# Attention of a hybrid decoder layer: where the far products with values stand, and in which order the four tiles of a group run

## The chip, the core and the metric

The kernel runs on one core of a Trainium2 chip. The time is the device time of one execution in microseconds; of several executions the median is given. The profile is one execution, recorded by the hardware profiler: for each engine it tells when each instruction ran, what it wrote and read, and what it had waited for. The engines are TensorE (PE; its weight loads are kept apart as PEld), VectorE (DVE), ScalarE (ACT), GpSimd (POOL), and SyncE (SP), which here only issues DMAs. Each engine takes its instructions in the order in which they were written for it, and an instruction that waits holds up everything behind it on its engine.

## The reference

One decoder layer on 2048 tokens and 1024 channels: attention heads and pooling groups side by side, then a gated MLP, then a gated embedding, then a last normalisation. The change touches the attention alone: 8 heads of 64 channels, and for each head three dilated patterns whose outputs are mixed by their softmax denominators.

```
DIL_PATTERNS = ((128, 1), (512, 4), (2048, 16))      # (window, dilation)
...
    s = jnp.einsum('bnqrhd,bnkrhd->bnrhqk', qb, kk)
    ...
    s = s - slopes[:, None, None] * dist
    s = jnp.where(valid[:, None, None], s, -jnp.inf)
    m = jnp.max(s, axis=-1, keepdims=True)
    e = jnp.exp(s - m)
    den = jnp.sum(e, axis=-1)
    o = jnp.einsum('bnrhqk,bnkrhd->bnqrhd', e, vv)
    ...
w = d * jnp.exp(m - jnp.max(m, axis=0, keepdims=True))
w = w / jnp.sum(w, axis=0, keepdims=True)
return jnp.sum(w[..., None] * o, axis=0)
```

## The kernel before

The program has three phases: projections, attention, and the rest. All of the change lies in `phase_attention`.

The attention is worked off in 128 **steps**: 8 heads of 16 query tiles of 128 rows. Four tiles make a **group**, which shares one residue of the dilation by 4; a group has a far part (the two long patterns at once) and a near part (the short one). Tile i of a group (i from 0 to 3) sees i + 1 blocks of 128 far keys, so its far scores are 128, 256, 384 or 512 wide; its near scores are 256 wide (128 for the first tile of a head). In float32 each score is made of two products: `qhh` (upper part of the query) and `qll` (lower part).

For a step s, this happens, each item on one engine:

- `near_scores` (N) and `far_scores` (F): two PE products each, into `sn` and `sf`. The stationary operand of the near products is a run of 128 queries, that of the far products every fourth query (`t.qr`, `t.qlr`).
- `near_max`, `far_max` (nm, fm): DVE adds the distances and takes the row's extreme, from `sn` and `sf` into `tt`.
- `near_exp`, `far_exp` (ne, fe): ACT takes the exponentials, from `tt` into `ee`.
- `turn` (T): PE transposes `ee` block by block (near and far, 3 to 6 blocks) into `tp`.
- `high` (h): ACT copies `tp` into `pth`; `low` (l): DVE takes the remainder `tp` - `pth` into `ptl`.
- `values`, `values_b` (V, W): PE multiplies `pth` and `ptl` of a whole group with the values `v`, in four parts: far parts 0 and 1 (`far_pv`), near parts 2 and 3 (`near_pv`), each split in two halves V and W. Block kb of the far part is (4 - kb) x 128 wide: 512, 384, 256, 128.
- `fold` (o) on ACT copies the far output out of `o`, `folded` (p) on DVE the near one.

What is written for the engines in one pass of the step loop is set by a table of names and lags. In pass s, the item with lag k works for step s - k:

```
'ord': [B 0, G 0, M 0, h 2, N 0, F 0, nm 0, p 7, o 8, ne 0, V 6, fm 0, l 2, W 6, S 1, fe 0, T 1]
```

So in pass s PE gets N(s), F(s), the values V and W of six steps ago, and then T(s - 1); DVE gets nm(s), at times a copy p, then fm(s), then l(s - 2); ACT gets h(s - 2), at times a copy o, then ne(s), fe(s). All engines follow this written order; no planner reorders it. `CFG['perm']` tells which tile i of its group a step takes:

```
st.n = n = n - n % 4 + CFG["perm"][n % 4]
st.r, st.i = divmod(n, 4)
st.nb, st.nf = min(n, 1) + 1, st.i + 1
```

The accumulators lie in PSUM. `sf` has two buffers, `o` two, and `sn` one bank with two halves. `tp` comes from two pools of **one buffer each**, chosen by the number of far blocks:

```
def turn(s):
    st = steps[s]
    if st.nf > 2:
        st.tp = ps_t.tile([P, 1024], F32, tag="t", name="tp")
    else:
        st.tp = ps_t.tile([P, CH], F32, tag="u", name="tp")
```

A buffer may be written again once all that read it have done so: for `tp` that is h on ACT and l on DVE. Once for each of the first three pairs of heads, `mix_stats` (S, at lines 795 and 798) also takes a buffer of the tag "t", under the name `tps`.

Of the kernel before, what the change touches and what calls it, by code (L numbers as in the profile page):

```python
# [20 lines left out]
S = 2048  # L21
# [19 lines left out]
V_N = V_CB + 2 * NF  # L41


CFG = {"tt": 2, "ee": 2, 'ord': [['B', 0], ['G', 0], ['M', 0], ['h', 2], ['N', 0], ['F', 0], ['nm', 0], ['p', 7], ['o', 8], ['ne', 0], ['V', 6], ['fm', 0], ['l', 2], ['W', 6], ['S', 1], ['fe', 0], ['T', 1]], 'perm': [3, 1, 2, 0], 'fp': [[0], [1], [2], [3]], 'np': [[0, -1], [1], [2], [3]], 'm': [9, 10, 13, 4, 6, 7]}


class Shared:
# [444 lines left out]
def phase_attention(tc, g, mx, near_b, far_b):  # L492
# [4 lines left out]
    NS = H * NQ  # L497
    LAST = 4 * H - 2
    with ExitStack() as ctx:
# [6 lines left out]
        heads, steps, groups, pairs = {}, {}, {}, {}  # L506
# [35 lines left out]
        def begin(s):  # L542
# [7 lines left out]
            st = steps[s] = Shared()  # L550
            st.n = n = n - n % 4 + CFG["perm"][n % 4]
            st.t, st.pt, st.e = heads[h], pairs[h // 2], h % 2
# [5 lines left out]
            st.d1, st.d3 = st.pt.st1[:, 1, st.e, n : n + 1], st.pt.st3[:, st.r, 1, st.e, st.i : st.i + 1]  # L558
            st.tt = sb.tile([P, 768], F32, tag="tt", bufs=CFG["tt"], name="tt")
            st.ee = sb.tile([P, 768], F32, tag="ee", bufs=CFG["ee"], name="ee")  # L560

        def far_scores(s):
            st = steps[s]
            t = st.t
            st.fv = ps_f.tile([P, CH], F32, tag="f", name="sf")[:, : st.wf]
            keys = t.ks[:, : st.nf, st.r, :]
            cl = slice(st.i * P, (st.i + 1) * P)
            nc.tensor.matmul(st.fv, t.qr[:, st.r, cl], keys, start=True, stop=False)
            nc.tensor.matmul(st.fv, t.qlr[:, st.r, cl], keys, start=False, stop=True)

        def near_scores(s):
            st = steps[s]
            t, n = st.t, st.n
            if s == 0:
                near_bank.append(ps_n.tile([P, CH], F32, tag="n", name="sn"))
            st.nv = near_bank[0][:, (s % 2) * 256 : (s % 2) * 256 + st.wn]
            keys = tokens(t.ks, n) if st.nb == 1 else two_tiles(t.ks, n)
            qs = slice(n * P, (n + 1) * P)
            nc.tensor.matmul(st.nv, t.qhh[:, qs], keys, start=True, stop=False, skip_group_check=True)
            nc.tensor.matmul(st.nv, t.qll[:, qs], keys, start=False, stop=True, skip_group_check=True)  # L580
# [48 lines left out]
        def near_pv(gi, kbs, first):  # L629
            gr, q0 = groups[gi], 4 * (gi % 4)  # L630
            for kb in kbs:
                if q0 + kb < 0:
                    continue
                m0, m1 = max(0, kb), min(3, kb + 1)
                b0, b1 = 4 * m0 + kb + 1, 4 * m1 + kb + 1
                kt = q0 + kb
                for pt in (gr.h, gr.l):
                    nc.tensor.matmul(
                        gr.o[1][:, m0 * P : (m1 + 1) * P],
                        vals[gi // 8, "v1", kt // 4][:, kt % 4, gi // 4 % 2, :],  # L640
                        pt[:, b0 : b1 + 1 : 4, :],
                        start=first,
                        stop=False,
                        skip_group_check=True,
                    )
                    first = False

        def far_pv(gi, kbs, first):
            gr = groups[gi]
            for kb in kbs:  # L650
                for pt in (gr.h, gr.l):
                    nc.tensor.matmul(
                        gr.o[0][:, kb * P :],
                        vals[gi // 8, "v3", gi % 4][:, kb, gi // 4 % 2, :],
                        pt[:, 6 * kb + 2 : 18 + kb : 5, :],
                        start=first,
                        stop=False,
                        skip_group_check=True,
                    )
                    first = False  # L660

        sums = Ticker()

        def halves(pt, gi, near):
            h, q = divmod(gi, 4)
            e = h % 2
            mine = slice(DH * e, DH * e + DH)
            other = slice(DH * (1 - e), DH * (1 - e) + DH)
            return e, mine, other, pt.s1[:, q * CH : (q + 1) * CH] if near else pt.s3[:, q, :]
# [17 lines left out]
        def shifts(s):  # L687
            sums.tick()

        def values(v):  # L690
            gi, part = v // 4, v % 4
            gr = groups[gi]
            if part % 2 == 0:
                gr.__dict__.setdefault("o", []).append(ps_o.tile([P, CH], F32, tag="o", name="o"))
            if part < 2:
                far_pv(gi, CFG["fp"][2 * part], part == 0)
            else:
                near_pv(gi, CFG["np"][2 * part - 4], part == 2)

        def values_b(v):  # L700
            gi, part = v // 4, v % 4
            if part < 2:
                far_pv(gi, CFG["fp"][2 * part + 1], False)
            else:
                near_pv(gi, CFG["np"][2 * part - 3], False)

# [50 lines left out]
        with tc.manual_schedule(engines=set(EN.values())):  # L757
            for dst, src in load_qk(0):
                rdma(nc, dst, src)
            for q in range(4):  # L760
                for which in ("v3", "v1"):
                    rdma(nc, *load_v(0, which, q))
            queue = []
            stages = {
                "F": far_scores, "N": near_scores, "fm": far_max, "nm": near_max, "fe": far_exp, "ne": near_exp,
                "T": turn, "h": high, "l": low, "V": values, "W": values_b, "S": stats, "M": mix, "o": fold, "p": folded, "B": begin, "G": shifts
            }
            for s in range(NS + 10):
                if s < NS:
                    h, n = divmod(s, NQ)  # L770
# [1174 lines left out]
def tile_layer(ctx, tc, xT, pT, vec, w_in, pool_w, w_out, w_up, w_down, w_gate, w_ple, near_b, far_b, rcnt, outT, upto=9):  # L1945
# [44 lines left out]
    with tc.manual_schedule(engines={mybir.EngineType.PE}):  # L1990
        with tc.manual_schedule(engines={EN[e] for e in ACFG["man"]}):
            phase_project(tc, g, xT, w_in, pool_w, rcnt)
        if upto > 1:
            mxs = ExitStack()
            mx = mxs.enter_context(tc.tile_pool(name="b_mx", bufs=1, side="right", reuse_waits="tile"))
            last = phase_attention(tc, g, mx, near_b, far_b)
            if upto > 2:
                phase_rest(tc, g, mxs, mx, last, xT, pT, w_out, w_up, w_down, w_gate, w_ple, outT)
            else:
                mxs.close()  # L2000
# [71 lines left out]
```

## Time and profile before

| | |
|---|---|
| median of 3 runs | 2359.09 us (2354.91 to 2359.45) |
| profiled execution | 2356.13 us, span 2354.1 us |
| attention, first score product to last value product | 387.3 to 637.3 us, 250 us |
| in it: PE busy | 241.51 us |
| ACT busy | 227.83 us |
| DVE busy | 218.46 us |
| POOL busy | 143.74 us |
| mean granted TensorE clock in it | 0.99 |

"Busy" counts an instruction from its start to its end, so overlapping starts and ends on PE and ACT make an engine look a little fuller than it is. In rows of the timeline the first number is the start in microseconds from the start of the span, the second the duration; in square brackets stands how long the engine had been idle before, and what ended that.

### The profile page before, as it was taken

How to read it: one execution, taken by the hardware profiler on the slowest of the kernel's cores; microseconds unless marked ns; L12 is line 12 of the kernel's file. 1: busy time of each engine (PE TensorE's matmuls, PEld its weight loads, DVE VectorE, ACT ScalarE, POOL GpSimd, SP SyncE). 2: the span in 40 equal slices, each digit the busy share in tenths (PEclk: the TensorE clock that was granted, in tenths of full speed). 3: DMA queues.
4: the chain of work that ended last, by engine and by line, in shares of the span. 5: the costliest groups of instructions: out<-in, count | busy, mean ns of one | idle time of the engine just before them, and what ended most of it. 6: DMA issues, size and time to landing. Idle time of an engine off the chain costs nothing.

```text
span 2354.1 us, 32813 instructions
## 1 busy us (share of the span) xinstructions
PE 2307.5 (98%) x11279; PEld 1955.0 (83%) x11279; DVE 1697.9 (72%) x2663; ACT 1125.0 (48%) x2044; POOL 571.9 (24%) x568
## 2 busy tenths in 40 slices
PE   8999999999899999999999999999999999999998
PEld 7988888999878878888887888888778888888888
DVE  6735436888863778999999999777765656655665
ACT  5423325999821344445446444444454544544332
POOL 2312221367600233333330665000110000001000
PEclk9999999999999999999999999999999999999999
DMA  8635446778764764555667777444496776754332
GB/s 263 209 121 192 152 157 236 249 242 272 225 235 156 251 209 151 200 192 194 205 199 258 272 275 249 154 137 152 167 344 223 253 230 199 236 161 148 119 103 95
DMA packets 237575, 476.00 MB, mean 202 GB/s; under 512 B 34400, under 2 KB 60832, under 8 KB 234336
## 3 DMA queue, kind: packets, MB, share of 16 engines
q1 hardware_dynamic: 205040, 394.64, 50.8%
q0 software_dynamic: 15888, 51.69, 6.2%
q10 hardware_dynamic: 16480, 27.58, 3.3%
q8 instruction: 89, 1.46, 0.3%
q14 instruction: 78, 0.64, 0.1%
HBM read 309.14 MB, written 156.79 MB: 198 GB/s over the span
## 4 chain that ended last, share of the span: by engine, by line
PE 86%; DVE 5%; DMA 4%; issue 2%; ACT 2%; POOL 1%; SPq 0%; DVEq 0%; POOLq 0%; ACTq 0%
PE ua L1405 18%; PE uc L1405 9%; PE dn L90 5%; PE dn L89 5%; PE dn L91 5%; PE z L89 5%; PE z L90 5%; PE z L91 5%; PE ub L1405 5%; PE o L91 2%; PE o L89 2%; PE o L90 2%; PE tp L610 2%; PE gp L89 2%; PE gp L90 2%
## 5 line engine op out<-in xcount | busy, mean ns | idle before, releaser
L90 PE MATMUL dn<-al,wu 128*128 128x512 f32 x616 | 240.3, 390 | 2.4 <-DVE al L85 2.4
L89 PE MATMUL dn<-ah,wu 128*128 128x512 f32 x616 | 240.4, 390 | 0.2
L91 PE MATMUL dn<-ah,wu 128*128 128x512 f32 x616 | 239.8, 389 | 0.0
L85 DVE TENSOR_TENSOR al<-ra,ah 128x512 fp32r<-128x512 f32 x154 | 105.7, 689 | 111.4 <-ACT ah L84 111.1
L89 PE MATMUL z<-hnh,wh 128*128 128x512 f32 (+1 forms) x480 | 168.4, 351 | 7.9 <-ACT hnh L258 6.2
L90 PE MATMUL z<-hnl,wh 128*128 128x512 f32 (+1 forms) x480 | 167.9, 350 | 0.1
L91 PE MATMUL z<-hnh,wl 128*128 128x512 f32 (+1 forms) x480 | 167.5, 349 | 0.0
L84 ACT CAST ah<-ra 128x512 fp32r<-128x512 f32 x154 | 95.2, 621 | 147.1 <-PE dn L91 137.6
L90 PEld LDWEIGHTS dn<-al,wu 128*128 128x128 f32 x616 | 115.6, 188 | 27.8 <-DVE al L85 4.1
L89 PEld LDWEIGHTS dn<-ah,wu 128*128 128x128 f32 x616 | 115.6, 188 | 25.4 <-ACT ah L84 1.3
L91 PEld LDWEIGHTS dn<-ah,wu 128*128 128x128 f32 x616 | 115.6, 188 | 23.9
L85 DVE TENSOR_TENSOR wu<-ru,wu 128x1024 fp32r<-128x1024 f32 x88 | 135.0, 1534 | 0.0
L1405 PE MATMUL ua<-s4h,wu 128*128 128x512 f32 x352 | 118.4, 398 | 0.0
L1405 PE MATMUL uc<-s3h,wu 128*128 128x512 f32 x352 | 116.7, 392 | 1.5 <-ACT s3h L1461 1.5
L1405 PE MATMUL ua<-s2h,wu 128*128 128x512 f32 x352 | 116.1, 391 | 1.7 <-ACT ug L1607 1.5
L1405 PE MATMUL ua<-s1h,wu 128*128 128x512 f32 x352 | 115.7, 389 | 1.6 <-ACT ug L1633 1.6
L1405 PE MATMUL ua<-a11h,wu 128*128 128x512 f32 x352 | 115.7, 390 | 0.0
L1405 PE MATMUL uc<-a22h,wu 128*128 128x512 f32 x352 | 115.6, 389 | 0.0
L1405 PE MATMUL ub<-a12h,wu 128*128 128x512 f32 x352 | 115.5, 389 | 0.0
L85 DVE TENSOR_TENSOR wu<-rw,wu 128x512 fp32r<-128x512 f32 x149 | 100.8, 685 | 20.1 <-ACT wu L84 19.8
L155 DVE TENSOR_TENSOR acc<-acc,sq 128x512 f32<-128x512 f32 (+1 forms) x118 | 79.1, 670 | 41.8 <-ACT sq L154 30.5
L89 PEld LDWEIGHTS z<-hnh,wh 128*128 128x128 f32 x480 | 92.4, 192 | 20.0 <-ACT hnh L258 6.2
(339 smaller groups left out, 6638.6 us busy)
## 6 DMA issues: line engine op xcount, KB each, us to landing
ru<-in_w_up_dram SPq DMA_DIRECT2D x66, 512.0 KB, 4.2
wr<-in_w_in_dram SPq DMA_DIRECT2D x64, 256.0 KB, 5.0
rw<-in_w_down_dram SPq DMA_DIRECT2D x61, 256.0 KB, 4.2
nt<-h SPq DMA_DIRECT2D x56, 256.0 KB, 3.9
td<-t SPq DMA_DIRECT2D x22, 512.0 KB, 2.6
t<-td SPq DMA_DIRECT2D x22, 512.0 KB, 3.7
nt<-in_w_down_dram POOLq DMA_DIRECT2D x44, 256.0 KB, 5.6
ra<-oq0s SPq DMA_DIRECT2D x44, 256.0 KB, 3.5
```

The costliest lines, as they stand in the source:

```text
L84: nc.scalar.copy(hi, src)
L85: (low or nc.gpsimd).tensor_tensor(lo, src, fp(hi), op=ALU.subtract)
L89: nc.tensor.matmul(ps, wh, ah, start=first, stop=False, skip_group_check=again)
L90: nc.tensor.matmul(ps, wh, al, start=False, stop=False, skip_group_check=again)
L91: nc.tensor.matmul(ps, wl, ah, start=False, stop=last, skip_group_check=again)
L155: nc.vector.tensor_tensor(acc[:, :n], acc[:, :n], sq[:, :n], op=ALU.add)
L610: nc.tensor.transpose(st.tp[:, bs], st.ee[:, bs], g.ident)
L1405: nc.tensor.matmul(pst, x[:, ksl], y, start=first and k == 0 and n == 0, stop=k == HK - 1 and n == 2, skip_group_check=True)
```

## The change

The diff does three things. First, the order of the four tiles: `perm` was 3, 1, 2, 0 and is now 3, 2, 0, 1. By the step's number modulo 4 the far scores were 512, 256, 384, 128 wide and are now 512, 384, 128, 256 wide, and the `tp` buffers, which went t, u, t, u, now go t, t, u, u. Second, the far value blocks are paired anew: part 0 had the blocks of 512 and 384 columns, part 1 those of 256 and 128; now part 0 has 512 and 128, part 1 has 384 and 256. Third, the V half of a far part no longer stands at its own place behind F: its two products are written between those of F, value, score, value, score.

```diff
-'perm': [3, 1, 2, 0], 'fp': [[0], [1], [2], [3]],
+'perm': [3, 2, 0, 1], 'fp': [[0], [3], [1], [2]],
...
         def far_scores(s):
...
+            v = s - 6
+            with_values = 0 <= v < NS and v % 4 < 2
+            between = values(v, True) if with_values else iter(())
+            next(between, None)
             nc.tensor.matmul(st.fv, t.qr[:, st.r, cl], keys, start=True, stop=False)
+            next(between, None)
             nc.tensor.matmul(st.fv, t.qlr[:, st.r, cl], keys, start=False, stop=True)
+            if with_values:
+                assert next(between, None) is None
+                taken.add(v)
...
         def far_pv(gi, kbs, first):
...
                     first = False
+                    yield True
...
-        def values(v):
+        def values(v, steps=False):
+            if v in taken:
+                return
             gi, part = v // 4, v % 4
...
             if part < 2:
-                far_pv(gi, CFG["fp"][2 * part], part == 0)
+                it = far_pv(gi, CFG["fp"][2 * part], part == 0)
+                if steps:
+                    return it
+                list(it)
```

Since V and W have a lag of 6, far part 0 falls on steps with s modulo 4 = 2, and part 1 on those with 3. `turn` itself is as before.

On PE, a step with remainder 2 in the middle of head 1, from its near scores to the transposes of the step ahead of it. Before:

```order
L579 MATMUL sn_4007<-ks1_4019,qhh1_4017 128x256 [waits DVE_49]
L580 MATMUL sn_4007<-ks1_4019,qll1_4018 128x256
L568 MATMUL sf_4542<-ks1_4019,qhh1_4017 128x384
L569 MATMUL sf_4542<-ks1_4019,qll1_4018 128x384
L652 MATMUL o_4550<-pth_4432,v3_0_0_3985 128x512 [waits Activation_49]
L652 MATMUL o_4550<-ptl_4433,v3_0_0_3985 128x512 [waits DVE_49]
L652 MATMUL o_4550<-pth_4432,v3_0_0_3985 128x384
L652 MATMUL o_4550<-ptl_4433,v3_0_0_3985 128x384
L610 MATMUL tp_4558<-ident_60,ee_4508 128x128 [waits PE_49,Activation_49]
```

and now:

```order
L587 MATMUL sn_4007<-ks1_4019,qhh1_4017 128x256 [waits DVE_49]
L588 MATMUL sn_4007<-ks1_4019,qll1_4018 128x256
L660 MATMUL o_4543<-pth_4432,v3_0_0_3985 128x512 [waits Activation_49]
L572 MATMUL sf_4542<-ks1_4019,qhh1_4017 128x128
L660 MATMUL o_4543<-ptl_4433,v3_0_0_3985 128x512 [waits DVE_49]
L574 MATMUL sf_4542<-ks1_4019,qll1_4018 128x128
L660 MATMUL o_4543<-pth_4432,v3_0_0_3985 128x128
L660 MATMUL o_4543<-ptl_4433,v3_0_0_3985 128x128
L618 MATMUL tp_4558<-ident_60,ee_4508 128x128 [waits DVE_49,PE_49]
```

The values now stand around the scores, the scores are the narrowest instead of the second widest, and the first transpose, which waited for PE and ACT, now waits for DVE.

On DVE, the items of that step and of the one behind it (`ISA` is nm or fm; its row with `128x1` reads the extreme out). Before:

```order
L584 ISA tt_4991,st1_4803<-sn_4007,nb2_4399 128x256 [waits DVE_49,PE_49]
L584 ISA st1_4803 128x1
L676 COPY ev_5003<-o_4948 128x512 [waits DMAHW5_49,Pool_49]
L590 ISA tt_4991,st3_4804<-sf_4999,fb2_4400 128x384 [waits PE_49]
L590 ISA st3_4804 128x1
L627 TENSOR_TENSOR ptl_4995<-tp_4982,pth_4994 128x768 [waits Activation_49]
L584 ISA tt_5021,st1_4803<-sn_4007,nb2_4399 128x256 [waits DVE_49,PE_49]
L584 ISA st1_4803 128x1
L590 ISA tt_5021,st3_4804<-sf_5027,fb2_4400 128x128 [waits PE_49]
L590 ISA st3_4804 128x1
L627 TENSOR_TENSOR ptl_4995<-tp_5015,pth_4994 128x512 [waits Activation_49]
```

and now:

```order
L592 ISA tt_4991,st1_4802<-sn_4007,nb2_4399 128x256 [waits DVE_49,PE_49]
L592 ISA st1_4802 128x1
L686 COPY ev_5006<-o_4946 128x512 [waits DMAHW5_49,Pool_49]
L598 ISA tt_4991,st3_4803<-sf_4999,fb2_4400 128x128 [waits PE_49]
L598 ISA st3_4803 128x1
L635 TENSOR_TENSOR ptl_4995<-tp_4982,pth_4994 128x768 [waits Activation_49]
L592 ISA tt_5022,st1_4802<-sn_4007,nb2_4399 128x256 [waits DVE_49,PE_49]
L592 ISA st1_4802 128x1
L598 ISA tt_5022,st3_4803<-sf_5028,fb2_4400 128x256 [waits PE_49]
L598 ISA st3_4803 128x1
L635 TENSOR_TENSOR ptl_4995<-tp_5015,pth_4994 128x640 [waits Activation_49]
```

DVE's order of items is as it was; only the widths follow the tiles. The last item of the first step (its sixth row) reads `tp` of the tile with four far blocks (768 columns), as before.

On PE, the end of a step with remainder 0: the last near values, then the transposes. Before:

```order
L638 MATMUL o_4493<-ptl_4323,v1_0_2_3995 128x128
L638 MATMUL o_4493<-pth_4322,v1_0_3_3999 128x256
L638 MATMUL o_4493<-ptl_4323,v1_0_3_3999 128x256
L610 MATMUL tp_4503<-ident_60,ee_4460 128x128 [waits DVE_49,PE_49,Activation_49]
L610 MATMUL tp_4503<-ident_60,ee_4460 128x128 [waits Activation_49]
```

and now:

```order
L646 MATMUL o_4491<-ptl_4323,v1_0_2_3995 128x128
L646 MATMUL o_4491<-pth_4322,v1_0_3_3999 128x256
L646 MATMUL o_4491<-ptl_4323,v1_0_3_3999 128x256
L618 MATMUL tp_4501<-ident_60,ee_4461 128x128 [waits DVE_49,PE_49]
L618 MATMUL tp_4501<-ident_60,ee_4461 128x128
```

The work ahead of the transposes is the same. The transposes' buffer was "u", last used two steps before, and is "u" again, now last used one step before.

More of the change, by code (lines that the diff above doesn't have):

```diff
@@ L41 @@
 V_N = V_CB + 2 * NF
-CFG = {"tt": 2, "ee": 2, 'ord': [['B', 0], ['G', 0], ['M', 0], ['h', 2], ['N', 0], ['F', 0], ['nm', 0], ['p', 7], ['o', 8], ['ne', 0], ['V', 6], ['fm', 0], ['l', 2], ['W', 6], ['S', 1], ['fe', 0], ['T', 1]], 'perm': [3, 1, 2, 0], 'fp': [[0], [1], [2], [3]], 'np': [[0, -1], [1], [2], [3]], 'm': [9, 10, 13, 4, 6, 7]}
+CFG = {"tt": 2, "ee": 2, 'ord': [['B', 0], ['G', 0], ['M', 0], ['h', 2], ['N', 0], ['F', 0], ['nm', 0], ['p', 7], ['o', 8], ['ne', 0], ['V', 6], ['fm', 0], ['l', 2], ['W', 6], ['S', 1], ['fe', 0], ['T', 1]], 'perm': [3, 2, 0, 1], 'fp': [[0], [3], [1], [2]], 'np': [[0, -1], [1], [2], [3]], 'm': [9, 10, 13, 4, 6, 7]}
 class Shared:
@@ L660, in far_pv @@
                     first = False
+                    yield True
         sums = Ticker()
+        taken = set()
         def halves(pt, gi, near):
@@ L702, in values_b @@
             if part < 2:
-                far_pv(gi, CFG["fp"][2 * part + 1], False)
+                list(far_pv(gi, CFG["fp"][2 * part + 1], False))
             else:
```

## The prediction

> **What bounds the kernel now.** I read the page first, then the attention's stretch by engine, then PE's, DVE's and PEld's timelines of one group.
>
> ```profile
> PE 2307.5 (98%) x11279; PEld 1955.0 (83%) x11279; DVE 1697.9 (72%) x2663; ACT 1125.0 (48%) x2044; POOL 571.9 (24%) x568
> 387.30:637.30 250.00, 241.51 (x1673) 232.25 (x1671) 218.46 (x694) 227.83 (x679) 143.74 (x139) 0.99 0.80 253
> ```
>
> PE is busy nearly all the time, in the attention too (241.51 of 250 us), but there DVE and ACT stand close behind. So a gain on PE counts at once, and a wait of PE on DVE costs at once. I call the steps by their number modulo 4 (step 2, 3, 0, 1), and a step's tile by the same number. One group on PE:
>
> ```profile
> 421.03 0.36 PE L579 MATMUL sn<-ks,qhh 128*128 128x256 f32 x1
> 421.23 0.28 PE L580 MATMUL sn<-ks,qll 128*128 128x256 f32 x1
> 421.35 0.45 PE L568 MATMUL sf<-ks,qhh 128*128 128x384 f32 x1
> 421.64 0.40 PE L569 MATMUL sf<-ks,qll 128*128 128x384 f32 x1
> 421.87 0.40 PE L652 MATMUL o<-pth,v 128*128 128x512 f32 x1
> 422.34 0.34 PE L652 MATMUL o<-pth,v 128*128 128x384 f32 x1
> 422.70 0.60 PE L610 MATMUL tp<-ident,ee 128*128 128x128 f32 x4
> ...
> 423.05 0.30 PE L579 MATMUL sn<-ks,qhh 128*128 128x128 f32 x1
> ...
> 424.73 0.37 PE L579 MATMUL sn<-ks,qhh 128*128 128x256 f32 x1
> ...
> 425.40 0.39 PE L569 MATMUL sf<-ks,qll 128*128 128x512 f32 x1
> 425.63 0.28 PE L638 MATMUL o<-pth,v 128*128 128x256 f32 x1
> ...
> 426.32 0.38 PE L610 MATMUL tp<-ident,ee 128*128 128x128 f32 x2
> 426.46 0.36 PE L579 MATMUL sn<-ks,qhh 128*128 128x256 f32 x1
> ...
> 427.24 0.28 PE L638 MATMUL o<-pth,v 128*128 128x256 f32 x1
> ...
> 427.66 0.84 PE L610 MATMUL tp<-ident,ee 128*128 128x128 f32 x6
> 428.26 0.36 PE L579 MATMUL sn<-ks,qhh 128*128 128x256 f32 x1
> ```
>
> Steps 2, 3, 0, 1 begin at 421.03, 423.05, 424.73, 426.46; the next group at 428.26. A group takes 7.23 us, and PE waits nowhere in it (the other groups of a head differ by a tenth or so). Streaming costs 0.235 us for 512 columns (two in 421.87 to 422.34), 0.18 for 384, so 0.12 for 256 and 0.06 for 128. Six transposes take 0.60 up to the next `sn`, four 0.35: 0.12 a block, so 0.49 for five and 0.25 for three. The weight loads set a floor:
>
> ```profile
> 423.25 0.31 PEld L568 LDWEIGHTS sf<-ks,qhh 128*128 128x128 f32 x1
> 423.46 0.33 PEld L569 LDWEIGHTS sf<-ks,qll 128*128 128x128 f32 x1
> 423.69 0.21 PEld L652 LDWEIGHTS o<-pth,v 128*128 128x128 f32 x1
> 423.82 0.19 PEld L652 LDWEIGHTS o<-ptl,v 128*128 128x128 f32 x1
> ```
>
> The far queries (every fourth) hold the loader 0.21 to 0.23 us from start to start, a plain load 0.12 to 0.13. A load runs under the product before it, so each product follows the one ahead of it by the longer of that one's streaming and its own load. I take 0.235 for a far load and 0.12 for a plain one.
>
> **What the change takes off PE.** From the second `sn` product to the transposes, by that rule. Step 2 before: 0.235 + 0.235 + 0.18 for the scores, then two times 0.235 and two times 0.18: 1.48 (the rows: 422.70 - 421.23 = 1.47). Now: value 0.12, score 0.235 (loaded under the 512-wide value), value 0.12, score 0.235, then three times 0.12: 1.05. Step 3: 0.235 + 0.235 + 0.12 x 5 before (the last score and four short values), 1.05 now, nothing gained. Step 1: its far scores grow from 256 to 384, 0.06 more. The sum is 0.42 - 0.06 = 0.36 a group on PE. With 31 of the 32 groups under the new pairing (the last one's values have no score products left beside them) this would be 11 us, if nothing else moved.
>
> A page speaks against it. The Trainium skill, "TensorE: Matmul & The Clock Gate", section "LDWEIGHTS (loading the stationary operand)", counts only the columns, an estimate of 107 ns for 128. By that a far load costs no more than another, alternating hides nothing and the 11 us would be 0; the rows above (0.31 and 0.33 against 0.19) disagree, and I go by them.
>
> **What it puts on the path.** The `tp` buffers. They alternated t, u, t, u, so that a transpose into one found it last used two steps before. Now they go t, t, u, u. T of tile 1 stands at the end of step 2 and needs "t" back from tile 0, whose l stands on DVE in that same step, behind nm, the copy p and fm. T of tile 3, at the end of step 0, needs "u" back from tile 2, whose l stands in step 0 behind nm and fm. Behind a waiting T stand N and F of the next step, and for these DVE waits. DVE's items, from rows:
>
> ```profile
> 428.78 0.42 DVE L584 CUSTOM_DVE_ANT_0 tt<-sn,nb 128x256 f32<-128x256 f32 x1 [0.49 <-PE sn L580]
> 429.13 0.69 DVE L676 COPY ev<-o 128x512 f32<-128x512 f32 x1
> 429.73 0.55 DVE L590 CUSTOM_DVE_ANT_0 tt<-sf,fb 128x384 f32<-128x384 f32 x1
> 430.20 0.95 DVE L627 TENSOR_TENSOR ptl<-tp,pth 128x768 fp32r<-128x768 f32 x1
> ...
> 431.41 0.29 DVE L590 CUSTOM_DVE_ANT_0 tt<-sf,fb 128x128 f32<-128x128 f32 x1
> 431.62 0.69 DVE L627 TENSOR_TENSOR ptl<-tp,pth 128x512 fp32r<-128x512 f32 x1
> ...
> 433.05 0.69 DVE L590 CUSTOM_DVE_ANT_0 tt<-sf,fb 128x512 f32<-128x512 f32 x1
> 433.67 0.82 DVE L627 TENSOR_TENSOR ptl<-tp,pth 128x640 fp32r<-128x640 f32 x1
> ```
>
> From start to start: nm 0.35, copy 0.60, fm 0.47 for 384, 0.62 for 512, 0.21 for 128 (so 0.34 for 256); l, its record less 0.08: 0.87 for 768, 0.61 for 512, 0.74 for 640, so 0.48 for 384. DVE starts 0.20 after a score's last column. The trace of before holds this very wait three times, where `tps` takes "t" one step after tile 2 did:
>
> ```profile
> 447.90 0.28 PE L638 MATMUL o<-ptl,v 128*128 128x256 f32 x1
> 449.10 0.27 PE L795 MATMUL tps<-ident,st 128*64 128x128 f32 x1 [0.93 <-DVE ptl L627]
> 447.52 0.69 DVE L590 CUSTOM_DVE_ANT_0 tt<-sf,fb 128x512 f32<-128x512 f32 x1
> 448.13 0.82 DVE L627 TENSOR_TENSOR ptl<-tp,pth 128x640 fp32r<-128x640 f32 x1
>   DVE ptl L627: 2.8, 3
> ```
>
> PE was ready at 448.02 and went on at 449.10, 0.15 after l's end: 1.08 us lost, behind the same 512-wide fm that step 0 has.
>
> I walk one group, t = 0 at step 2's first `sn`. *Step 2:* second `sn` 0.20; nm 0.52, copy 0.87, fm (scores done long before) 1.47, l of 768 1.68 to 2.63. T could start at 0.20 + 1.05 = 1.25 and starts at 2.78: **1.53 lost**. Five blocks, step 3 at 3.27. *Step 3:* DVE, idle since 2.55, has nm at 3.79; the second far score ends streaming at 4.29, fm 4.49, l of 640 4.83 to 5.57. T needs no late buffer: 3.47 + 1.05 = 4.52, three blocks, step 0 at 4.77. *Step 0:* nm at 5.57 (DVE late), scores streamed by 5.68, fm 5.92, l of 384 6.54 to 7.10. Near values end 0.69 after the scores (425.63 to 426.32): T could start at 6.37 and starts at 7.25: **0.88 lost**. Four blocks, step 1 at 7.60. *Step 1:* second `sn` 7.80, scores 0.235 + 0.235 + 0.18, near values 0.42 (427.24 to 427.66), T at 8.87, six blocks, next group at 9.47. DVE is done with fm (8.65 to 9.12) and l of 512 by 9.73, before the next nm at 9.99.
>
> ACT does not add to it: in step 2 it has h, `ne` and `fe`, and
>
> ```profile
> 429.01 0.79 ACT L623 CAST pth<-tp 128x768 fp32r<-128x768 f32 x1
> ```
>
> h of 768, begun when step 1's ACT items are done (about 0.45), ends near 1.25, ahead of l at 1.68. Its 227.83 us of 250 are spread over a third more time.
>
> So 9.47 against 7.23, **+2.24 a group**: 2.41 of waiting, 0.36 off PE, and the rest is that DVE, itself idle while T holds up the next N, comes late to step 0. For 31 groups this is 69 us. Off it go 3 us, since the three `tps` waits are then paid by T anyhow, and about 5 for stalls of before that a slower pace covers (the 1.60 below with its aftermath). Net +61: 2356.1 + 61 = 2417; the median stands 3 us above the profiled execution, so **2420 us**. For the unknown, the walk's latencies, I take 0.3 us a group either way, 10 us: 2408 to 2432.
>
> **Rivals.** *1, faster: no transpose waits.* If DVE had given the buffers back in time, the 11 us on PE would stand: 2348. For it speaks PE's 98%; against it the three `tps` rows and DVE's written order, which puts l behind fm. It decides only if l ends before T is ready, in step 2 that is 1.53 us earlier than walked.
>
> *2, slower still: the clock.* Some gaps of PE cost a stretch at half clock, others none:
>
> ```profile
> 588.77 0.39 PE L579 MATMUL sn<-ks,qhh 128*128 128x256 f32 x1 [1.60 <-DVE st L584]
> 590.00:592.00 2.00, 2.00 (x12) 1.86 (x10) 1.81 (x4) 2.00 (x6) 0.10 (x1) 0.57 1.03 335
> 47.51 0.50 PE L90 MATMUL z<-wl,hnh 128*128 128x512 f32 x1 [1.52 <-DVE wl L85]
> ```
>
> The gap of 1.60 was followed by a clock of 0.57, that of 1.52 was not, and the 0.93 ones were not. Step 2's gap, about 1.4 as a record, lies between. If it counts where it falls whole into one interval of the watcher (some 3.4 us, by the length of the slow stretch), that is 55% of 31 groups, 17 times about 1.5 us (3.4 us at 0.57 lose 0.43 of it): +25, 2445. The Trainium skill, same page, section "Why this matters for your kernels", allows gaps up to about 3 us; by that this rival falls away and 2420 stands, but the 1.60 row shows the limit lower.
>
> *3, only one wait costs.* If step 0's wait is hidden, because fm there starts on time, 0.88 x 31 = 27 us go: 2393. Against it: the `tps` wait stands in that very step.
>
> *4, the alternation itself fails*, its values waiting for `pth` or `ptl` since they stand earlier. The first `ptl` product needs l of step 1's pass, whose record ends at 9.81, so it could start at 9.96; it stands 0.67 into the next step 2 (0.20 + 0.12 + 0.235 + 0.12), at 10.14: 0.18 to spare. If it fell away, T's wait would hide it, and 2420 holds.
>
> **How the numbers follow.** The forecast (with 4) has 0.63, the clock 0.25, one wait 0.06, no wait 0.06. The likeliest gives 2420. For 8 in 10 the range takes its 2408 to 2432, most of the clock's case and the upper part of the third: 2400 to 2450. A difference under 0.2% (4.7 us, the spread of the runs of before) can't be told from none. Slower by more than that are the first three, 0.93; no change would need waits of about 0.36 a group, 0.01; faster 0.06.
>
> **What would show it.** Right: PE idle before `tp` released by DVE's `ptl`, some 60 times, near 1.4 and 0.7 us as records; groups of about 9.4 us; DVE waiting for `sn` in steps 3 and 1; score and value products starting about 0.12 and 0.24 apart. Wrong: `tp` without idle time and groups of 6.9; one of the two waits missing; or the clock in the attention well under 0.99 (rival 2).

## The result

The changed kernel takes 2414.35 us (median of 4 runs, 2410.84 to 2414.53) against 2357.0 us for the kernel before (4 runs, 2354.83 to 2359.45): 1.0254 times as long, with a 95% interval of 1.024 to 1.0268, or 57 us more. The forecast was 2420 us (2356 for the profiled execution of before, 61 for the groups, and 3 by which the median then stood above that execution), with a range of 2400 to 2450.

### The profile page after: what moved, and what is told of

Read it like the earlier page. It is cut to its first block, busy times and chain, and to the rows that moved or that the text cites. A ratio compares the mean times of both kernels' runs of the same rounds, so it can differ in the third digit from the quotient of the medians.

```text
span 2412.6 us, 32746 instructions
## 1 busy us (share of the span) xinstructions
PE 2307.4 (96%) x11279; PEld 1952.8 (81%) x11279; DVE 1698.4 (70%) x2663; ACT 1136.6 (47%) x2044; POOL 572.4 (24%) x568
## 4 chain that ended last, share of the span: by engine, by line
PE 82%; DVE 9%; issue 4%; DMA 3%; ACT 2%; SPq 0%; POOL 0%; DVEq 0%; POOLq 0%; ACTq 0%
PE ua L1420 18%; PE uc L1420 9%; PE dn L90 5%; PE dn L91 5%; PE dn L89 5%; PE ub L1420 5%; PE z L90 4%; PE z L89 4%; PE z L91 4%; PE tp L618 3%; DVE ptl L635 2%; PE o L91 2%; PE o L89 2%; PE o L90 2%; PE gp L89 2%
## 5 line engine op out<-in xcount | busy, mean ns | idle before, releaser
L618 PE MATMUL tp<-ident,ee 128*128 128x128 f32 x568 | 88.0, 282 | 70.1 <-DVE ptl L635 66.6
L618 PEld LDWEIGHTS tp<-ident,ee 128*128 128x128 f32 x568 | 63.0, 143 | 80.3 <-issue 78.6
```

The lines of the kernel that those rows point to most:

```text
L618: nc.tensor.transpose(st.tp[:, bs], st.ee[:, bs], g.ident)
```

## The profile after

The page of the changed kernel, its first lines:

```profile
span 2412.6 us, 32746 instructions
PE 2307.4 (96%) x11279; PEld 1952.8 (81%) x11279; DVE 1698.4 (70%) x2663; ACT 1136.6 (47%) x2044; POOL 572.4 (24%) x568
```

The span is 58.5 us longer, and PE is busy as long as it was (2307.4 against 2307.5 us). DVE and POOL are too, and ACT's records grow by 11.6 us. So PE has no more work; it waits more. Who waits, from the list of waits between 400 and 690 us (waiting engine and line, released by; us in total, times, the longest):

```profile
PEld tp L618 <- issue: 71.0, 57, 1.8
DVE tt L592 <- PE sn L588: 69.8, 82, 1.9
PE tp L618 <- DVE ptl L635: 60.1, 53, 1.7
```

Before, the largest wait of PE on DVE between 400 and 620 us was 2.8 us in three times, ahead of `tps`; no `tp` waited for `ptl`. Now the transposes (`tp`) wait for DVE's `ptl` 53 times in this stretch of 31 groups, close to twice a group, and DVE then waits for the next `sn`. Over the whole attention the view of the tile `tp` has:

```profile
  issue: 78.6, 61
  DVE ptl L635: 66.6, 57
...
  DVE lo L908: 2.8, 3
```

60 waits, 69.4 us of recorded idle time ("issue" is the weight loads' share of the same waits, and `lo` at L908 is an item right behind an l, named because it ended last). One step with remainder 2 on PE, and DVE in the same step:

```profile
479.52 0.37 PE L587 MATMUL sn<-ks,qhh 128*128 128x256 f32 x1
479.72 0.28 PE L588 MATMUL sn<-ks,qll 128*128 128x256 f32 x1
479.84 0.40 PE L660 MATMUL o<-pth,v 128*128 128x512 f32 x1
480.08 0.22 PE L572 MATMUL sf<-ks,qhh 128*128 128x128 f32 x1
480.14 0.45 PE L660 MATMUL o<-ptl,v 128*128 128x512 f32 x1
480.43 0.22 PE L574 MATMUL sf<-ks,qll 128*128 128x128 f32 x1
480.48 0.28 PE L660 MATMUL o<-pth,v 128*128 128x128 f32 x1
480.60 0.27 PE L660 MATMUL o<-ptl,v 128*128 128x128 f32 x1
482.30 0.74 PE L618 MATMUL tp<-ident,ee 128*128 128x128 f32 x5 [1.43 <-DVE ptl L635]
482.79 0.36 PE L587 MATMUL sn<-ks,qhh 128*128 128x256 f32 x1
```

```profile
480.04 0.42 DVE L592 CUSTOM_DVE_ANT_0 tt<-sn,nb 128x256 f32<-128x256 f32 x1 [0.18 <-PE sn L588]
...
480.39 0.69 DVE L686 COPY ev<-o 128x512 f32<-128x512 f32 x1
480.99 0.28 DVE L598 CUSTOM_DVE_ANT_0 tt<-sf,fb 128x128 f32<-128x128 f32 x1
...
481.20 0.95 DVE L635 TENSOR_TENSOR ptl<-tp,pth 128x768 fp32r<-128x768 f32 x1
483.32 0.42 DVE L592 CUSTOM_DVE_ANT_0 tt<-sn,nb 128x256 f32<-128x256 f32 x1 [1.16 <-PE sn L588]
```

PE has done its products by 480.72 and stands until 482.30, 0.15 after l ends at 482.15. DVE in its turn has nothing to do from there to 483.32, since the next `sn` is queued behind the waiting transposes. The value product now hides most of a far load: the two `o` of 512 and the two `sf` of 128 take 479.84 to 480.48, 0.64 us, where two far scores of 384 alone took 0.52 before (421.35 to 421.87).

The second wait, at the end of step 0 of the next group:

```profile
495.25 0.28 PE L646 MATMUL o<-ptl,v 128*128 128x256 f32 x1
496.23 0.63 PE L618 MATMUL tp<-ident,ee 128*128 128x128 f32 x4 [0.70 <-DVE ptl L635]
496.62 0.36 PE L587 MATMUL sn<-ks,qhh 128*128 128x256 f32 x1
```

PE has done its products by 495.37 and goes on at 496.23, 0.15 after l of 384 columns, which runs on DVE from 495.53 to 496.08: 0.86 us lost.

All 31 groups from step 2 of the first group on, as the times between the first `sn` of one step with remainder 2 and that of the next (read from the timeline):

| | median group | sum of 31 groups |
|---|---|---|
| before | 7.34 us | 234.4 us |
| after | 9.48 us | 296.3 us |

## The experiments

Each run below was timed beside runs of the kernel before on the same chip. That kernel's median was 2353 to 2354 us there, so ratios are compared, and differences in microseconds are worked out from the ratio times 2357.

**The order of the tiles alone.** The kernel before with one number table changed:

```diff
-'perm': [3, 1, 2, 0], 'fp': [[0], [1], [2], [3]]
+'perm': [3, 2, 0, 1], 'fp': [[0], [1], [2], [3]]
```

> The kernel before with the new order of the four tiles alone; pairing and place of the value products are as before. Theory (the late tp buffer costs the time): l of tile 0 ends in step 2 at the same moment as in the changed kernel (nm, copy, fm, l on DVE: T at 2.78 into the step), the PE work ahead of it is only longer and hidden in the wait, step 0 is the same: groups of 9.4 to 9.5 us, time within 4 us of the changed kernel's 2414. Rival (the alternation brings the far scores later to DVE and makes the values wait): without it groups near 7.3 us, 2357 to 2362.

Measured: 2409.56 us, ratio 1.0241 (1.0226 to 1.0256); groups of 9.40 us (median). The view of `tp` in this kernel:

```profile
  issue: 70.3, 61
  DVE ptl L627: 54.3, 59
```

59 waits on DVE's `ptl` without any alternation: the order of the tiles carries the loss. The alternation and the new pairing on top of it add 0.08 us to the median group and 0.0013 to the ratio, within both intervals.

**The old order, with the alternation and the new pairing.**

```diff
-'perm': [3, 2, 0, 1], 'fp': [[0], [3], [1], [2]]
+'perm': [3, 1, 2, 0], 'fp': [[0], [3], [1], [2]]
```

> The changed kernel with the old order of tiles, so the tp buffers alternate t, u, t, u again; the alternation and the new pairing stay. Theory: no transpose waits. PE step 2 falls from 1.47 to 0.12 + 0.235 + 0.18 + 0.235 + 0.18 + 0.12 + 0.12 = 1.19 us behind the second sn, step 3 and step 1 stay: 0.28 a group, 31 times, 8.7 us off: 2346 to 2351. Rival (the alternation costs): 2380 or more.

Measured: 2351.91 us, ratio 0.9992 (0.9982 to 1.0001): the 57 us are gone, so the alternation is not their cause, but the 8.7 us did not come either; no difference from before can be told. The median group is 7.17 us, 0.17 under before instead of 0.28. PE's step 2 did get shorter (1.11 us from the second `sn` to the transposes, 1.19 expected). In step 3 the transposes of tile 2 then come up against ACT:

```profile
439.16 0.52 ACT L604 ACTIVATE ee<-tt,st 128x256 f32<-128x256 f32 x1
439.57 0.20 ACT L604 ACTIVATION_READ_ACCUMULATOR ee<-tt,st 128x1 f32 x1
439.66 0.61 ACT L608 ACTIVATE ee<-tt,st 128x384 f32<-128x384 f32 x1
440.17 0.20 ACT L608 ACTIVATION_READ_ACCUMULATOR ee<-tt,st 128x1 f32 x1
440.26 0.57 ACT L631 CAST pth<-tp 128x512 fp32r<-128x512 f32 x1
```

ACT runs without a gap, its far exponentials end at 440.37, and PE's transposes, ready about 440.45 by its rows, start at 440.55. The profile also holds one group of 11.36 us, where before had 8.98. The 31 groups together take 230.8 us, 3.6 under before; yet the last near value product comes at 637.1 us, as before (637.2), because in this profile the attention begins 3.0 us later (first `sn` at 390.55 against 387.55). So the groups did get shorter, by less than half of what was expected, and the times of the runs show nothing beyond their spread.

**Two wide tp buffers (two_wide_tp).** The changed kernel with a second `tp` buffer and nothing moved; one `sf` buffer pays for it:

```diff
-        ps_f = ... tc.tile_pool(name="b_f", bufs=2, ...)
+        ps_f = ... tc.tile_pool(name="b_f", bufs=1, ...)
...
-            if st.nf > 2:
-                st.tp = ps_t.tile([P, 1024], F32, tag="t", name="tp")
-            else:
-                st.tp = ps_t.tile([P, CH], F32, tag="u", name="tp")
+            st.tp = ps_t.tile([P, 1024], F32, tag="t", bufs=2, name="tp")
```

(the last statistics, which had used `sf`'s buffers, take those of `tp`.)

> The changed kernel with two tp buffers of two banks under one tag for all tiles, paid for by one sf buffer instead of two (the last statistics use tp's buffers then). A transpose needs its buffer back from two steps before, as in the kernel before; F needs fm of the step before, which by the walk is done 0.2 to 0.8 us ahead. Theory: the waits of T go, the 0.36 us a group on PE come to light, groups of 6.9 us, 11 us under before: 2345 to 2350. Rival (the alternation costs): 2400 or more. If the single sf buffer makes F wait instead, PE shows idle time before sf released by DVE's st.

Measured: 2349.21 us, ratio 0.998 (0.9971 to 0.999): 0.2% under before, and the loss of the changed kernel is gone. Of its waits between 400 and 620 us, those of PE on DVE, and the largest of DVE on PE:

```profile
DVE tt L592 <- PE sn L588: 6.8, 36, 0.3
...
PE sn L587 <- DVE st L592: 2.5, 1, 2.5
...
PE tp L615 <- DVE ptl L632: 0.2, 1, 0.2
PE o L657 <- DVE ptl L632: 0.2, 1, 0.2
```

So the late buffer is the cause: give the transposes a second one and the loss is gone, with the order and the alternation as they are. The gain is 4.7 us and not 11. The median group is 7.16 us (0.18 under before). The groups with four instead of six near value products in step 0 are at 6.77 against 7.11, the full 0.34. In those of 7.16 the chain runs over ACT: its items stand end to end, h in step 2 ends at 435.89 and l begins at 435.92, DVE ends fm of the step behind it at 437.55, and the load for F in step 0, which needs the single `sf` buffer back, begins at 437.62, 0.11 later than behind `sn` otherwise. Two groups take 9.51 and 9.47 us; there PE waits once for `st`, the 2.5 us above. The attention's last value product comes at 630.3 us, 6.9 earlier than before. About 2 of these are lost behind it, where the output projection waits for its weights and the clock stands at half longer:

```profile
635.53 0.80 PE L89 MATMUL o<-mh,hwo 128*128 128x512 f32 x1 [4.94 <-ACT hwo L84]
639.25 0.80 PE L91 MATMUL o<-mh,lwo 128*128 128x512 f32 x1 [2.50 <-DVE lwo L85]
```

In the profile before the same two rows stood at 642.92 and 645.32, 2.40 us apart instead of 3.72, and the first `wb` product behind them stood at 654.64; now it is at 649.66, 5.0 us earlier and not 6.9.

**The near copy behind l.** The changed kernel with one item moved in DVE's order:

```diff
-['nm', 0], ['p', 7], ['o', 8], ['ne', 0], ['V', 6], ['fm', 0], ['l', 2], ['W', 6]
+['nm', 0], ['o', 8], ['ne', 0], ['V', 6], ['fm', 0], ['l', 2], ['p', 7], ['W', 6]
```

> The changed kernel with one item moved in DVE's order: the near copy (p) stands behind l instead of ahead of fm and l. Theory: in step 2 l of tile 0 ends 0.60 us earlier, T goes with it, the copy falls into the time in which DVE waits for the next sn; step 0 is as it was. 31 times 0.60 us: 18.6 us under the changed kernel, 2393 to 2399. Rival (T waits for something other than DVE's chain, ACT's h or the scores): no change, 2411 to 2417.

Measured: 2406.59 us, ratio 1.0223 (1.0208 to 1.0238), 7 us under the changed kernel and not 18.6. The group went from 9.48 to 9.17 us. DVE in step 2, which begins at 485.93:

```profile
486.45 0.42 DVE L592 CUSTOM_DVE_ANT_0 tt<-sn,nb 128x256 f32<-128x256 f32 x1 [0.17 <-PE sn L588]
...
487.09 0.29 DVE L598 CUSTOM_DVE_ANT_0 tt<-sf,fb 128x128 f32<-128x128 f32 x1 [0.21 <-PE sf L574]
...
487.31 0.95 DVE L635 TENSOR_TENSOR ptl<-tp,pth 128x768 fp32r<-128x768 f32 x1
488.18 0.68 DVE L686 COPY ev<-o 128x512 f32<-128x512 f32 x1
```

With the copy gone from ahead of it, fm waits for the scores, which the alternation had put later: the second `sf` stands behind a long product now and ends about 0.96 into the step. So fm starts at 1.16 (487.09 less 485.93) and not at 0.87, l ends 0.30 earlier and not 0.60, and T goes with it (488.41, 2.48 into the step, against 2.78). The direction is the theory's; the expectation had left out the second thing that fm waits for. 31 times 0.30 is 9.3 us; the 31 groups of the two profiles differ by 7.6.

**A second narrow buffer alone.** The changed kernel with the tag u doubled, t single:

```diff
-                st.tp = ps_t.tile([P, CH], F32, tag="u", name="tp")
+                st.tp = ps_t.tile([P, CH], F32, tag="u", bufs=2, name="tp")
```

(with one `sf` buffer, as above.)

> The changed kernel with a second buffer of the narrow tag u alone (tag t stays single; one sf buffer pays for it). Theory: the wait of step 2 (for t) stays, that of step 0 (for u, 0.88 us by the walk) goes: groups of 8.6 instead of 9.48 us, 27 us under the changed kernel, 2384 to 2392. Rival (DVE is the bound of the whole group, and the wait taken away in step 0 comes back in another step): less than 10 us gained.

Measured: 2390.32 us, ratio 1.0164 (1.0148 to 1.018): 21 us under the changed kernel by the ratios. The view of `tp`:

```profile
  issue: 53.2, 33
  DVE ptl L635: 49.4, 32
```

32 waits instead of 57: one a group is left, of 1.5 us. The groups are at 8.76 us (median), 0.72 under 9.48, where the walk's 0.88 had been expected. So there are two waits, each with a cost of its own: about 0.7 us a group goes with the narrow buffer, and the rest stays with the wide one, whose wait is now 1.43 us in some groups and up to 1.73 in others. A second wide buffer by itself was not run.

**Two wide buffers in the kernel before.** The same buffers, the old order, no alternation.

> The kernel before with the buffers of the run two_wide_tp: two wide tp buffers, one sf buffer, old order, no alternation. Theory (the 5 us of two_wide_tp come from the alternation on PE): no gain, groups of 7.3 us as before, or up to 0.1 a group lost where F waits for the single sf buffer: 2353 to 2360. Rival (they come from the second tp buffer): 2349 as two_wide_tp.

Measured: 2352.6 us, ratio 0.9999 (0.9989 to 1.0009), groups of 7.34 us: no gain from a second buffer can be told where the order alternates, and none is lost by the single `sf` buffer. So the 4.7 us of two_wide_tp come with what it has besides, the new order and the alternation; the two intervals just touch.

**The pairing alone.** The kernel before with `'fp': [[0], [3], [1], [2]]`.

> The kernel before with the new pairing of the far value blocks alone. By PE's rows step 2 gets 0.11 us shorter (two products of 0.18 us become two of 0.12) and step 3 as much longer: the group is the same. Theory and rival both: 2353 to 2358, unless the ACT or DVE work of the longer step 3 stands closer to PE there (then up to 0.1 a group more).

Measured: 2353.34 us, ratio 1.0002 (0.9994 to 1.0011), groups of 7.33 us: nothing.

**Two wide buffers, order 3, 2, 1, 0.**

> The run two_wide_tp with the order 3, 2, 1, 0: far scores 512, 384, 256, 128. PE's sum is the same (both narrow scores still stand between long values). Theory (in two_wide_tp ACT and DVE, not PE, are now the nearer bound: ACT without idle time in the groups of 7.16 us): within 3 us of two_wide_tp, 2346 to 2352. If PE's order alone counted: the same 2349.

Measured: 2350.13 us, ratio 0.9987 (0.9976 to 0.9997). The median group is 7.01 us, 0.33 under before: nearly all of the 0.36 that was worked out for PE. The 31 groups take 226.0 us, 8.4 under before, and this profiled execution was the shortest of the twelve (2345.75 us). The others go up to 2355.71, and what they lose no profile here shows. Even in the profiled one two groups take 9.64 and 9.77 us. There DVE's first item of the mixing waits for a load, PE waits behind it, and the clock stands at 0.50 from 523 to 529 us:

```profile
522.04 0.78 DVE L905 TENSOR_TENSOR lo<-sn,sf 128x32 f32<-128x32 f32 x1 [2.74 <-DMA sf<-stf]
523.22 0.58 PE L587 MATMUL sn<-ks,qhh 128*128 128x256 f32 x1 [2.57 <-DVE st L592]
```

**That item two steps later.** The last run with `if d == 11:` instead of `if d == 9:` ahead of `mix_lift`.

> The run two_wide_tp_3210 with one item of the mixing of a finished pair of heads (mix_lift, whose first instruction on DVE waits for a load) put two steps later, 11 instead of 9 steps behind the pair's end. In the profiles that wait costs DVE 2.7 us once (two_wide_tp_3210), PE then 2.6 us and a stretch at half clock, some 5 us in two groups of 9.7 instead of 7.0. Theory (the load is late by 1 to 3 us and two steps are 3.5 us): where it struck, 2 to 5 us go: 2344 to 2349, groups of 7.0 as before. Rival (the load lands later in step with the rest, or ACT's share waits next): 2349 to 2352.

Measured: 2358.56 us, ratio 1.0022 (1.0011 to 1.0033), 0.2% slower than before, where 2344 to 2349 had been expected. The wait of DVE is gone, but two groups take 14.06 and 14.25 us:

```profile
ACT wts L749 <- POOL ex L909: 11.4, 2, 5.8
PE o L657 <- ACT ev L683: 11.3, 3, 5.4
```

The differences `ex`, which POOL makes from `mix_lift`'s result, now stand behind additions that wait for transfers (`s` <- `ev`; in the first of these groups one ends its wait at 530.36, and `ex` comes at 532.23). ACT's `wts` waits 5.6 us for `ex`, and PE waits 5.25 us for the copies `ev` behind it.

## Why the prediction was right

**The walk of one group** held to a few hundredths. Predicted and measured lengths of the steps 2, 3, 0, 1 (the steps after begin at 479.52, 482.79, 484.30, 487.14 and 489.00):

| | step 2 | step 3 | step 0 | step 1 | group |
|---|---|---|---|---|---|
| predicted | 3.27 | 1.50 | 2.83 | 1.87 | 9.47 |
| measured | 3.27 | 1.51 | 2.84 | 1.86 | 9.48 |

T of tile 1 was to lose 1.53 us in step 2 and loses 1.58 (480.72 to 482.30); PE was there a little earlier than walked. T of tile 3 was to lose 0.88 in step 0 and loses 0.86 where step 0 has six near value products (495.37 to 496.23). That the wait is for the buffer, and not for the scores, ACT or the alternation, was argued in the prediction from three `tps` rows; the runs show it: the order alone brings it, a second narrow buffer takes its part away, and a second buffer for all tiles takes all of it away.

**The gain on PE** of 0.36 a group is real where nothing else stands beside it (0.33 with order 3, 2, 1, 0; 0.34 in the shorter groups of two_wide_tp). In the changed kernel the waits cover it, as the prediction had it. Rival 1's time for it, 11 us, was too large a promise: with the waits gone, 4.7 us were measured, and 2 us, not to be told from none, with the old order. What the prediction did not weigh there is that ACT has hardly any time left in a group of 7.1 us, as the rows of these two runs show.

**The sum** came out nearly right, in part by luck. 31 groups were to cost 2.24 us each, less 3 for `tps`, less 5 for stalls that a slower pace covers, 61 in all. Measured from the list of groups: 61.8, as 2.14 by the medians times 31, 66, less about 5 for the three groups with `tps` (8.98 us before, 9.47 to 9.49 after), less 3 for the two slow groups of before (8.96 and 8.72), and some 3 for two new slow ones. The two deductions were the wrong way round, their sum was right. The 2.24 was 0.1 too large because the group taken as the base, 7.23 us from 421.03, stands at a change of heads: it has near scores of 128 columns and a transpose of two blocks, and the median group took 7.34. Of the 0.19 that the prediction left to DVE's lateness in step 0 this is 0.11; that lateness was already counted in the 0.88.

Two more terms stood nowhere in the prediction. From the last group's end to the last value product the attention takes 14.5 us instead of 10.7, and it begins 0.4 later, so that product comes 66.0 us later (703.2 against 637.2), not 61.8. Behind it 7.5 us came back, down to the 58.5 of the span. The largest single part is PE's wait for the output projection's weights, 5.45 us before, which is

```profile
706.39 0.50 PE L89 MATMUL o<-mh,hwo 128*128 128x512 f32 x1 [2.90 <-ACT hwo L84]
```

2.90 us now.

**Rival 2, the clock,** came true in two full groups and not in 17. The wait of 1.43 us is in most groups and leaves the clock alone; two longer ones did not, of which the first is:

```profile
471.63 1.28 PE L618 MATMUL tp<-ident,ee 128*128 128x128 f32 x5 [1.74 <-DVE ptl L635]
471.40:475.20 3.80, 3.57 (x17) 3.60 (x18) 1.27 (x6) 1.59 (x4) 2.69 (x3) 0.55 0.79 296
```

The clock is 0.55 over these 3.8 us (0.50 for 3.4 of them), and those two groups take 11.05 and 10.44 us: 2.5 us in all, against the 25 of the rival. By the Trainium skill's rule ("TensorE: Matmul & The Clock Gate", section "Why this matters for your kernels", gaps up to about 3 us) they too should have been harmless; this trace agrees for the waits of 1.43 us and not for those of 1.74. A third wait of 1.73 us, ahead of 625.46, again left the clock at 1.00. The clock also stood at 0.50 from 396.5 to 403.4 in the first group, and from 697.0 to 700.3 behind the last. The first group took 9.79 us, against 8.33 with the order alone, whose clock stood at 1.00 there.

**Rivals 3 and 4** fell: both waits cost (a second narrow buffer took 21 us off), and the alternation's own products did not wait in step 2 (`o` at 479.84 follows `sn` by 0.12). Of what would show it, the waits, the groups of about 9.4 us and DVE's waits for `sn` are there. The starts of score and value products were told as 0.12 and 0.24 apart; they stand at 0.24, 0.06, 0.29, 0.05, the same sum less 0.07.

## What to carry to other kernels

A table that sets the order of work also decides which buffers are used back to back. Before such an order is changed, write down for each single buffer which item uses it next and when its last reader runs: here that one line (t, u, t, u to t, t, u, u) cost five times what the change on PE could bring. A second buffer, paid for with one that was hardly missed, took that cost away and left 4.7 us of the gain. A gain worked out for the busiest engine is only an upper bound where two others are over 85% busy, and the time it leaves must also be wanted by what comes next.

## What the runs showed of the hardware

A weight load of 128 x 128 whose columns are every fourth element of a row takes 0.31 to 0.33 us as a record against 0.19 for a plain one, and holds up the following product by about 0.23 us where the product ahead of it is shorter; a product of 512 columns ahead of it hides most of that (0.64 us for two such products and two far scores of 128).

The clock dropped to half for 3.4 us after idle times of 1.60 us (before) and 1.74 us (after, twice), and never after those of 1.43 us. The length of the gap alone does not decide: a third wait of 1.73 us in the changed kernel and several of 1.62 to 1.64 us with the second narrow buffer (ahead of 411.99 and 446.29) left the clock at 1.00. Where the gap falls in time seems to count as well. In the changed kernel the slow stretches begin at 396.55, 471.65, 550.15 and 696.95 us, which are 22, 23 and 43 times 3.41 us apart, and each lasts once or twice that time. What has to come together within such an interval no run here tells.
